# Releasing the store of one batch on its own data: the tail of a batched transposed matmul

## The chip, the cores and the metric

The kernel runs on one core of a Trainium2 chip. The metric is the device time of one execution in microseconds (us), as the median of several executions. The profiled execution has its own span, which is about 1.8 us shorter than the device time, as it begins and ends at the first and last instruction. All positions "at 112.2 us" are counted from the start of that span. PE is the matmul engine (PEld its weight loads), DVE and ACT copy and convert, SyncE (SP) and ACT issue transfers, and 16 DMA engines carry them out. A semaphore is a counter that one engine raises and another waits for. A store has landed when the last of its 16 parts has been confirmed.

## The reference

```python
batch, m, k, n = 16, 512, 512, 512          # a: (16, k, m), b: (16, n, k), float32
out = np.matmul(a.transpose(0, 2, 1), b.transpose(0, 2, 1)).astype(np.float32)
```

The inputs are 16.8 MB each and the output is 16.8 MB: 50.33 MB cross between HBM (the memory of the chip) and SBUF (the working memory of the core).

## The kernel before: the parts that matter

Each batch is multiplied on PE in two halves of two quarters; each finished quarter adds 1 to `summed`, so quarter q (from 0) of batch i brings it to 4*i + q + 1. DVE copies the first half out of PSUM (where PE accumulates), ACT the second. Batches are stored in pairs of 2 MB; only the last pair (batches 14 and 15) is stored as two transfers of 1 MB. The last three pairs are issued by SyncE:

```python
MO, B, H, TAIL = 4, 16, 8, 3
def run_sp(sp):
    ...                                            # cut: all loads
    for j in range(H - TAIL, H - 1):               # pairs 5 and 6
        sp.wait_ge(summed, MO * (2 * j + 2) + 3)
        store(sp, j)
    sp.wait_ge(summed, MO * (B - 1) + 3)           # third quarter of batch 15
    store(sp, H - 1, slice(0, 1))                  # batch 14
    sp.wait_ge(last_go, 3)                         # the three last copies
    store(sp, H - 1, slice(1, 2))                  # batch 15
```

Waiting for quarter 3 of the next batch is an indirect way of waiting for the copies: PE can begin the second half of batch 15 only when ACT has freed that accumulator.

```python
def run_act(act):
    cast_a(act, 0)
    for i in range(B - 1):
        cast_a(act, i + 1)
        copy_out(act, i, slice(2, 4), oa_go)       # oa_go: PE may reuse the accumulator
        ...                                        # cut: stores of the earlier pairs
    copy_out(act, B - 1, 2, last_go)
    copy_out(act, B - 1, 3, last_go)
```

## Time and profile before

| what | value |
|---|---|
| median of the first 3 runs | 124.81 us (124.78 to 124.95) |
| span of the profiled run | 123.1 us |
| PE, DVE, ACT busy | 70%, 46%, 38% |
| DMA share from 4.00 to 120.60 us | 1.01, at 426 GB/s |
| last three stores, issue | 108.26, 114.93, 116.46 us |

How to read it: no compute engine comes near 100%, while the DMA share stays at 1. The lines of the profile are shown in the prediction.

### The profile page before, as it was taken

The numbers are of one execution on the slowest core, as the hardware profiler recorded it, in microseconds if no ns is written. First come the engines' busy times: TensorE is split into PE (matmuls) and PEld (weight loads), VectorE is DVE, ScalarE is ACT, GpSimd is POOL, SyncE is SP. The second block draws the span as 40 slices with busy tenths as digits, with TensorE's granted clock in tenths as the row PEclk, the third lists the DMA queues.
The fourth block names the chain that finished last, engine by engine and source line by source line (L and its number), as shares of the span: only waits on it lengthen the run. The fifth ranks groups of instructions, "written<-read, shape, count | busy, mean of one in ns | idle before, by whom it ended". The sixth has DMA issues, their size and how long they took to land. (4 is left out here: it accounts for less than half of the span.)

```text
span 123.1 us, 1084 instructions
## 1 busy us (share of the span) xinstructions
PE 85.9 (70%) x400; PEld 49.6 (40%) x400; DVE 56.4 (46%) x48; ACT 46.8 (38%) x34; POOL 0.7 (1%) x6
## 2 busy tenths in 40 slices
PE   0007497997999799769932599965992679979600
PEld 0007354643754564436402336533550526447200
DVE  0025377469295665907049007780719306162100
ACT  4004209438617903276300860329230590740300
POOL 2000000000000000000000000000000000000000
PEclk9999999999999999999995558999999558999985
DMA  4999999999999999999999999999999999999993
GB/s 96 389 399 453 407 426 461 434 383 461 426 391 461 426 341 431 429 431 439 437 407 426 445 429 415 429 423 434 463 397 431 423 426 426 429 426 431 426 421 130
DMA packets 5648, 50.33 MB, mean 409 GB/s; under 512 B 528, under 2 KB 528, under 8 KB 528
## 3 DMA queue, kind: packets, MB, share of 16 engines
q1 hardware_dynamic: 4288, 39.85, 77.4%
q10 hardware_dynamic: 1360, 10.49, 20.1%
HBM read 33.55 MB, written 16.78 MB: 409 GB/s over the span
## 5 line engine op out<-in xcount | busy, mean ns | idle before, releaser
L215 PE MATMUL o_ps<-bt_sb,a_bf 128*128 128x512 bf16 x256 | 65.0, 402 | 7.8 <-PEq L190 7.3
L132 ACT CAST a_bf<-a_sb 128x2048 bf16<-128x2048 f32 x16 | 30.4, 1901 | 40.5 <-DMA a_sb<-in_a_dram 40.5
L215 PEld LDWEIGHTS o_ps<-bt_sb,a_bf 128*128 128x128 bf16 x256 | 28.5, 115 | 38.1 <-issue 15.7
L201 PE MATMUL bt_ps<-identity,b_bf 128*128 128x128 f32 x144 | 24.1, 322 | 22.2 <-PEq L190 22.2
L141 DVE COPY o_sb<-o_ps 128x1024 f32<-128x1024 f32 x16 | 19.6, 1224 | 36.5 <-PE o_ps L215 36.5
L201 PEld LDWEIGHTS bt_ps<-identity,b_bf 128*128 128x128 f32 x144 | 22.2, 212 | 27.6 <-issue 26.6
L149 DVE CAST b_bf<-b_sb 128x2048 bf16<-128x2048 f32 x16 | 19.5, 1222 | 18.5 <-DMA b_sb<-in_b_dram 18.5
L141 ACT COPY o_sb<-o_ps 128x1024 f32<-128x1024 f32 (+1 forms) x17 | 16.3, 962 | 28.2 <-PE o_ps L215 28.2
L158 DVE COPY bt_sb<-bt_ps 128x1024 f32<-128x1024 f32 x16 | 19.5, 1216 | 2.9 <-PE bt_ps L201 2.9
L132 ACT ACT_TABLE_LOAD x1 | 1.3, 1283 | 0.9 <-SPq L51 0.9
L119 POOL TENSOR_SCALAR_AFFINE_SELECT identity<-identity 128x128 f32<-128x128 f32 x1 | 0.3, 292 | 0.2 <-POOL identity L117 0.2
L117 POOL MEMSET identity<- 128x128 f32 x1 | 0.2, 204 | 0.7 <-SPq L51 0.7
L261 POOL MEMSET const-bfloat16-1.0<- 128x1 bf16 x1 | 0.1, 101 | 0.0
L261 POOL MEMSET const-uint8-127<- 128x1 uint8 x1 | 0.1, 101 | 0.0
L261 POOL MEMSET const-float32-0.0<- 128x1 f32 x1 | 0.1, 98 | 0.2 <-issue 0.2
L261 POOL MEMSET const-float32-1.0<- 128x1 f32 x1 | 0.1, 98 | 0.0
## 6 DMA issues: line engine op xcount, KB each, us to landing
b_sb<-in_b_dram SPq DMA_DIRECT2D x8, 2048.0 KB, 20.5
a_sb<-in_a_dram SPq DMA_DIRECT2D x16, 1024.0 KB, 17.4
out_dram<-o_sb ACTq DMA_DIRECT2D x5, 2048.0 KB, 15.2
out_dram<-o_sb SPq DMA_DIRECT2D x2, 2048.0 KB, 13.8
out_dram<-o_sb SPq DMA_DIRECT2D x2, 1024.0 KB, 5.1
```

Source lines behind the costliest of these rows:

```text
L117: pool.memset(identity[:], 0.0).then_inc(id_go, 1)
L119: pool.affine_select(out=identity[:], in_=identity[:], compare_op=mybir.AluOpType.not_equal, fill=1.0, base=0, pattern=[[-1, P]], channel_ ...
L132: act.copy(a_bf[i % 2][:], a_sb[s][:]).then_inc(ac_go, 1)
L141: copy(o_sb[i // 2 % OUTS][:, i % 2, rm, :], o_ps[h][:, p, :]).then_inc(go, 1)
L149: dve.tensor_copy(b_bf[:, r, :], b_sb[p % PAIRS][:, r, :]).then_inc(bc_go, n)
L158: dve.tensor_copy(bt_sb[g][:].rearrange("p j (ni r) -> p j ni r", r=NR), bt_ps[:].rearrange("p j r (g ni) -> p g j ni r", g=2)[:, g],).the ...
L201: last = pe.transpose(bt_ps[:, j, r, :], w[:, r, j, :], identity[:])
L215: last = pe.matmul(o_ps[h][:, q, :], a_r[:, rk, 2 * h + q, :], bt_h[:, rk // 2, rk % 2, :], start=(rk == 0), stop=(rk == KO - 1),)
L261: nc = _bacc.Bacc("TRN2", target_bir_lowering=False, num_devices=1)
```

## The change

The intent is to let batch 14's store go as soon as its two copies are done. ACT announces its copy with a drain (an instruction that here ended 0.035 us after the copy before it) and a semaphore. SyncE still waits for one PE count, the first quarter of batch 15, which stands for DVE's copy.

```diff
+        half_go = sem("half_go")
...
-            sp.wait_ge(summed, MO * (B - 1) + 3)
+
+            sp.wait_ge(summed, MO * (B - 1) + 1)
+            sp.wait_ge(half_go, 1)
             store(sp, H - 1, slice(0, 1))
...
+            act.drain().then_inc(half_go, 1)
             copy_out(act, B - 1, 2, last_go)
```

## The prediction

> **What bounds the kernel now.** I read the page from the top down: busy shares, slices, DMA queues, chain, groups. No compute engine is near full (PE 70%, DVE 46%, ACT 38% of 123.1 us). The DMA row of the slices is at 9 from the second slice to the last but one, and the total says why:
>
> ```profile
> PE 85.9 (70%) x400; PEld 49.6 (40%) x400; DVE 56.4 (46%) x48; ACT 46.8 (38%) x34; POOL 0.7 (1%) x6
> ...
> DMA  4999999999999999999999999999999999999993
> ...
> HBM read 33.55 MB, written 16.78 MB: 409 GB/s over the span
> ```
>
> The reader is to see that 50.33 MB have to cross the 16 DMA engines whatever the order, and that the engines hardly rest between the first slice and the last. Over the stretch from 4.00 to 120.60 us the table of windows gives a DMA share of 1.01 and 426 GB/s. 50.33 MB at 426 GB/s are 118.1 us; the remaining 5 us of the span are the start, before the first loads flow (131 GB/s in the half microsecond to 2 us, full rate from 3.5 us), and the end, when the last engines run out and the last store is confirmed. So the DMA is the bound.
>
> The chain that ended last shows only PE 5%: it goes back from the last copy on ACT to 109.97 us and stops there. It leaves out the transfers, so I don't take it as the bound. It is still useful, as it tells what sets the issue of the last store: PE, then ACT's two copies, ending at 115.85 + 0.58 = 116.43 us.
>
> Next the end in order of time (the timeline from 96 us on), as the change acts only there:
>
> ```profile
> 107.36 1.22 DVE L141 COPY o_sb<-o_ps 128x1024 f32<-128x1024 f32 x1 [2.47 <-PE o_ps L215]
> ...
> 109.17 1.01 ACT L141 COPY o_sb<-o_ps 128x1024 f32<-128x1024 f32 x1 [1.05 <-PE o_ps L215]
> ...
> 111.05 1.99 PE L215 MATMUL o_ps<-bt_sb,a_bf 128*128 128x512 bf16 x8
> ...
> 113.82 1.99 PE L215 MATMUL o_ps<-bt_sb,a_bf 128*128 128x512 bf16 x8
> ...
> 115.85 0.58 ACT L141 COPY o_sb<-o_ps 128x512 f32<-128x512 f32 x1 [0.32 <-PE o_ps L215]
> ```
>
> The reader is to see batch 14's output complete at 109.17 + 1.01 = 110.18 us, and the two halves of batch 15's matmuls starting at 111.05 and 113.82. The present store of batch 14 waits until the third quarter of batch 15's matmuls is done, about 113.82 + 1.99/2 = 114.82 us. The rows of the stores, asked for in small windows, place the SyncE issues at 108.26 (batches 12 and 13, 2 MB), 114.93 (batch 14, 1 MB) and 116.46 us (batch 15, 1 MB), with 8.9, 4.7 and 5.6 us to landing, thus landing at about 117.2, 119.6 and 122.1. So the store does sit idle after its data are ready, for 4.7 us. What decides is whether the DMA engines sit idle in that time. Windows of the end (columns: width, busy time of each engine, granted clock, DMA share, GB/s):
>
> ```profile
> 112.00:113.00 1.00, 1.00 (x7) 0.62 (x6) 0.00 (x0) 0.00 (x0) 0.00 (x0) 1.00 0.99 418
> 113.00:114.00 1.00, 1.00 (x10) 0.94 (x9) 0.93 (x1) 0.00 (x0) 0.00 (x0) 1.00 1.04 442
> 114.00:115.00 1.00, 1.00 (x6) 0.49 (x5) 0.30 (x1) 0.06 (x1) 0.00 (x0) 1.00 1.03 434
> 115.00:116.00 1.00, 0.81 (x4) 0.19 (x2) 0.00 (x0) 0.68 (x2) 0.00 (x0) 1.00 1.01 426
> 116.00:117.00 1.00, 0.00 (x0) 0.00 (x0) 0.00 (x0) 0.43 (x1) 0.00 (x0) 1.00 1.01 426
> 117.00:118.00 1.00, 0.00 (x0) 0.00 (x0) 0.00 (x0) 0.00 (x0) 0.00 (x0) 1.00 0.98 410
> ...
> 119.00:120.00 1.00, 0.00 (x0) 0.00 (x0) 0.00 (x0) 0.00 (x0) 0.00 (x0) 0.61 1.00 418
> 120.00:121.00 1.00, 0.00 (x0) 0.00 (x0) 0.00 (x0) 0.00 (x0) 0.00 (x0) 0.50 0.91 385
> 121.00:122.00 1.00, 0.00 (x0) 0.00 (x0) 0.00 (x0) 0.00 (x0) 0.00 (x0) 0.50 0.04 16
> ```
>
> The reader is to see that the share stays at 0.98 to 1.04 in every microsecond from 112 to 120, right through the late issue at 114.93. There is no hole for an earlier store to fill.
>
> **What the Trainium skill says.** "DMA: Bandwidth & Descriptors", section "Queues, rings and completion order", says that on each DMA engine the descriptors of one issuing queue are consumed in ring order. The trace agrees as far as landings can show it: the three last stores, all from SyncE, land in issue order, 2.4 to 2.5 us apart, and 1.049 MB in 2.45 us is 428 GB/s, the full rate. "HBM Reference", section "Specifications (TRN2)", says a core streaming alone gets about 425 GB/s, bounded by its 16 DMA engines; the trace's 426 agrees, so there is no faster rate to reach. "Perfetto Trace Analysis", section "DMA Instruction — HWDGE (DVE, Sync)", says that an issue's profiled time is not the data's movement and that the final semaphore write can be long delayed when the target is HBM. Here the issue takes 0.34 us against a landing 5.6 us later, and almost nothing moves after 121 us while the landing comes at 122.1; that confirmation of about a microsecond is not touched by the change.
>
> **The change part by part.**
>
> Removed: the wait for the third quarter of batch 15. In its place stands the wait for the first quarter of batch 15, which implies that DVE's copy of batch 14 is done, since PE can begin that half only when DVE has freed its accumulator. This quarter ends at 111.05 + 1.99/2 = 112.05. With the 0.11 us from matmul to issue that the old wait shows (114.82 to 114.93), the store goes out at about 112.16, that is 2.77 us earlier. It is not 4.7 us earlier, though the copies are done at 110.18, because the new count is also a PE count.
>
> Added: a drain on ACT with a semaphore increment. It begins when the copy of batch 14 ends at 110.18, and ACT's next work is at 114.94, after 4.76 us of idle time put down to PE. Whatever the drain costs under 4 us is hidden there. No row of this profile has its duration; I count 0 on the path. SyncE gets one more wait, met at about 110.3, before the other is.
>
> Moved: only that one issue. The issue of the last store, 116.46, hangs on ACT's last copy at 116.43, which hangs on PE. PE, DVE and ACT do nothing different before it. The order of the instructions on all engines, compared before and after, is the same but for the drain and the wait.
>
> The sum: at 114.93 the engines still have 0.03 + 0.426 + 0.426 + 0.410 + 0.434 + 0.418 + 0.385 + 0.016 = 2.545 MB to move (the windows' rates by their widths; 118 to 119 has 434). Two stores of 1.049 MB are 2.097 MB of it, so 0.448 MB, or 1.05 us at 426 GB/s, lie ahead of batch 14's store when it is issued. An issue needs about that much: the first one of the program, at 0.95 us, has data flowing in the half microsecond after 1.5. So the late issue arrives just in time. The earlier one meets 0.448 + 2.77 x 0.426 = 1.63 MB of backlog, waits 2.77 us longer in line, begins to move data at the same time as before, and lands at about 119.6 again, now 7.4 us after its issue. The last store follows it and lands at about 122.0. Expected saving: 0, with at most some tenths. The generous bound is to let the 0.98 of 117 to 118 become 1.01 and to let all 16 engines end together: 0.03 us, plus the 0.401 MB after 120 moved at 426 GB/s (0.94 us, to 120.94) instead of ending near 121.5. Neither is likely to be caused by the wait; I count 0.05 us.
>
> **The rivals.**
> 1. The store is on the path to the end, and 2.77 us come off (to about 122.0 us). For it: SyncE waits 21.9 us for PE in the end, 6.2 of them before this issue, and the last thing waited for is a store. Against it: the DMA share of 1.0 in those microseconds, and a last store that cannot issue before 116.46 and needs 1.049/0.426 = 2.46 us of transfer and the confirmation anyway.
> 2. A hole of some DMA engines that the mean share hides. Engines that finished their part of the 2 MB store early might have waited for the next one; then the earlier issue evens them out and up to 0.3 us come off. For it: 1.05 us of backlog is a thin margin. Against it: 410 to 442 GB/s throughout.
> 3. A new cost: the drain delays ACT, or two stores queued together slow loads or copies. Against it: 4.76 us of idle time on ACT, and the last load of `a` is already converted at 106.21, so no load is left to delay. It would add 0 to 0.3 us.
>
> **The range and the chances.** The three runs of before span 124.78 to 124.95, so repeats differ by 0.17 us. From 124.81 less 0.05 I predict 124.8 us. Rival 2 and the repeats set the low end at 124.4, rival 3 and another chip the high end at 125.2. Within 2% means 122.3 to 127.3, which no rival but the first leaves, and it needs the idle DMA time that the windows deny: faster 0.01, same 0.98, slower 0.01.
>
> **What would show each step right or wrong.** Right: the store of batch 14 issued near 112.2 with about 7.4 us to landing, the DMA share still 1.0 in each microsecond to 120, the last issue near 116.5 with 5.5 us to landing, ACT's last copies in place, span near 123.1. Wrong: a landing of batch 14's store well before 119 or of the last one before 121.5 (then there was a hole), a higher rate than 430 GB/s in the end, or ACT's copy after the drain starting late.

## The result, and the profile after

The changed kernel takes 124.85 us (median of 6 runs, 124.66 to 125.05), the kernel before 124.88 us in 6 runs beside and before them. The ratio is 0.9995 with a 95% interval of 0.9976 to 1.0015. Ratios here and below are the mean time of one kernel's fast runs over that of the other's fast runs of the same rounds, so they are not quite the ratio of the medians quoted. Executions over 1.5% slower than the fastest of the same kernel are left out of the means. The result is correct.

The page of the changed kernel, busy shares and DMA slices:

```profile
PE 86.1 (70%) x400; PEld 49.7 (40%) x400; DVE 56.4 (46%) x48; ACT 46.8 (38%) x34; POOL 0.7 (1%) x6
...
DMA  4999999999999999999999999999999999999992
```

The same picture as before: the busy shares are equal, and the DMA row is the same digit for digit but for the last slice. The timeline of the end:

```profile
109.27 1.01 ACT L144 COPY o_sb<-o_ps 128x1024 f32<-128x1024 f32 x1 [1.05 <-PE o_ps L219]
...
111.14 1.99 PE L219 MATMUL o_ps<-bt_sb,a_bf 128*128 128x512 bf16 x8
...
115.93 0.59 ACT L144 COPY o_sb<-o_ps 128x512 f32<-128x512 f32 x1 [0.32 <-PE o_ps L219]
```

Everything sits 0.1 us later than in the earlier trace and in the same order; ACT's last copy is not delayed by the drain. The waits of SyncE in the end (what waited, for whom: us in total, times, longest):

```profile
SPq L276 <- DMA out_dram<-o_sb: 4.6, 1, 4.6
SPq L86 <- ACT o_sb L144: 3.9, 1, 3.9
SPq L111 <- ACTq L188: 1.6, 1, 1.6
```

The third line is the new wait. It runs from the end of the issue before, 108.35 + 0.39 = 108.74, so it is met at about 110.3 (the trace's own row of this wait starts at 110.34), 0.06 us after ACT's copy ended at 109.27 + 1.01 = 110.28. The drain costs no more than that. The store then waits for the first quarter and is issued at 112.24 us, against 114.93 before. It needs 7.2 us to land instead of 4.7. Thus it lands at about 119.5 instead of 119.6, and the last store at 121.9 instead of 122.1. The DMA engines in this time (columns: stretch, width, busy time of PE, PEld, DVE, ACT and POOL, granted clock, DMA share, GB/s):

```profile
115.00:116.00 1.00, 0.89 (x4) 0.22 (x2) 0.00 (x0) 0.66 (x2) 0.00 (x0) 1.00 1.01 426
116.00:117.00 1.00, 0.00 (x0) 0.00 (x0) 0.00 (x0) 0.51 (x1) 0.00 (x0) 1.00 0.99 418
117.00:118.00 1.00, 0.00 (x0) 0.00 (x0) 0.00 (x0) 0.00 (x0) 0.00 (x0) 1.00 1.03 434
...
120.00:121.00 1.00, 0.00 (x0) 0.00 (x0) 0.00 (x0) 0.00 (x0) 0.00 (x0) 0.50 0.70 295
121.00:122.00 1.00, 0.00 (x0) 0.00 (x0) 0.00 (x0) 0.00 (x0) 0.00 (x0) 0.50 0.04 16
```

They were full before and are full now, until 120 us. The lower share after 120 (0.70 against 0.91) goes with an end 0.1 us earlier; the other two profiled runs of this kernel, e1_after and e12_again, end 0.15 us later and 0.14 us earlier than the kernel before, so no gain is to be read from it. The 2.7 us by which the store was issued earlier have become 2.5 us more in line.

### The profile page after: what moved, and what is told of

Read it like the earlier page. It is cut to its first block, busy times and chain, and to the rows that moved or that the text cites. A ratio compares the mean times of both kernels' runs of the same rounds, so it can differ in the third digit from the quotient of the medians.

```text
span 123.0 us, 1086 instructions
## 1 busy us (share of the span) xinstructions
PE 86.1 (70%) x400; PEld 49.7 (40%) x400; DVE 56.4 (46%) x48; ACT 46.8 (38%) x34; POOL 0.7 (1%) x6
```

## The experiments

The theory: at this point stores are waiting in line at full DMA engines, so the issue time of one more changes only how long it queues, until it comes so late that the line runs empty. Rivals: the issue bounds the end (every microsecond counts); single DMA engines have hidden holes that the earlier issue fills; the wait is felt nowhere at all. Twelve kernels ran, in four groups (sections 2 and 3 are one), each group with its own runs of the kernel before; only the last group, e12_again, was compared with the eleven runs of the group before it and one more.

### 1. Where the store is issued

The changed kernel was timed again (e1_after). In e2_copies the store waits for its two copies alone: DVE, too, announces its copy with a drain, after its last turn (the copy of transposed `b` that follows its copy of batch 14).

```diff
-            sp.wait_ge(summed, MO * (B - 1) + 1)
-            sp.wait_ge(half_go, 1)
+            sp.wait_ge(half_go, 2)
...
                 turn(p, 1)
+                if p + 1 == H:
+                    dve.drain().then_inc(half_go, 1)
```

> The changed kernel again, timed beside the other wait positions. Theory (the DMA engines always have a backlog at this point, so the issue only changes the wait in line): ratio to before 1.000, within 0.002; the store of batch 14 issued near 112.2 and landing near 119.5. Rival (hidden holes of single DMA engines, evened out by the earlier issue): a ratio of 0.997 to 0.999, clear of 1.

> The store waits for nothing but its two copies (no count of PE): issue near 110.4, 4.5 us before the old one. Theory: ratio 1.000 again, landing still near 119.5, some 9 us after the issue. Rival of hidden holes: at least as much gain as the changed kernel. Rival that the issue bounds the end: another 1.8 us off.

Two further kernels move the wait the other way, e3_fourth by one quarter and e4_with_last to the condition of the last store:

```diff
-            sp.wait_ge(summed, MO * (B - 1) + 3)
+            sp.wait_ge(summed, MO * (B - 1) + 4)    # e3_fourth
+            sp.wait_ge(last_go, 3)                  # e4_with_last
```

> The wait of before moved one quarter of matmuls later (fourth instead of third): issue near 115.95 instead of 114.93. Theory: the backlog of 1.05 us at 114.93 is used up near 116.0, and a store needs up to 1 us from issue to first data, so a hole of about 0.5 to 0.9 us opens and the time grows by that, to about 125.5. Rival that the wait is not felt at all: 124.85. Rival that every microsecond of the wait counts: plus 1.0.

> The store of batch 14 waits for the same count as the last store: issue near 116.5, 1.5 us later than before. Theory: first data near 117.4 against a backlog that ends near 116.0, so 1.4 us of hole and 126.2 us, ratio about 1.011; the windows show a DMA share well under 1 in 116 to 118. Rival that the wait is not felt: 1.000.

Issue and landing are those of each profiled run; the kernel before of this group had a median of 125.05 us (11 runs). One of the six runs of e4_with_last counts as slow and is left out of its ratio.

| kernel | issued | landed | DMA gap before its data | median us | ratio (95%) |
|---|---|---|---|---|---|
| e2_copies | 109.96 | 119.4 | none | 125.08 | 1.0008 (0.9982 to 1.0035) |
| e1_after | 110.82 | 119.8 | none | 124.76 | 0.9979 (0.9956 to 1.0002) |
| e3_fourth | 116.26 | 120.2 | 0.65 us | 125.15 | 1.0001 (0.9973 to 1.0028) |
| e4_with_last | 116.71 | 120.6 | 1.0 us | 126.13 | 1.006 (1.001 to 1.011) |

Between 110 and 115 us the issue time is worth nothing in these executions: the landing stays at 119.4 to 119.8, and going on from the changed kernel to the two copies alone gains nothing either. Later than that, the line runs empty. Windows of e3_fourth, then of e4_with_last (a packet is counted whole in the stretch in which it starts, so a short stretch can show a share over 1 and a GB/s figure that no engine reached):

```profile
115.00:116.00 1.00, 1.00 (x6) 0.39 (x4) 0.00 (x0) 0.58 (x1) 0.00 (x0) 1.00 0.80 336
116.00:116.50 0.50, 0.23 (x2) 0.00 (x0) 0.00 (x0) 0.23 (x1) 0.00 (x0) 1.00 0.05 16
116.50:117.10 0.60, 0.00 (x0) 0.00 (x0) 0.00 (x0) 0.35 (x1) 0.00 (x0) 1.00 0.00 0
117.10:117.30 0.20, 0.00 (x0) 0.00 (x0) 0.00 (x0) 0.00 (x0) 0.00 (x0) 1.00 1.58 655
```

```profile
116.55:117.55 1.00, 0.00 (x0) 0.00 (x0) 0.00 (x0) 0.14 (x1) 0.00 (x0) 1.00 0.00 0
```

Here one sees how close the old wait was. The engines begin to run out before 116 us and all stand still until 117.10, which is 0.84 us after the issue at 116.26. In e4_with_last they stand still from 116.55 to 117.55, again 0.84 us after the issue. Applied to the kernel before, data could start at 114.93 + 0.84 = 115.77 us (an estimate). The 16 parts of the store in front land from 116.27 to 117.11 us in that trace; as data ended 0.49 us before their landing in e3_fourth and e4_with_last, the DMA engines ran out of it from about 115.78 to 116.62 us (an estimate too). The late issue was thus in time for the first of them, with nothing to spare.

A later issue is felt less than this suggests. Against the kernel before, the store is issued 1.33, 1.78 and 2.36 us later in e3_fourth, e4_with_last and e10_late_pe_before (section 4). The 16 parts of the last store land 1.08, 1.54 and 2.11 us later on average, so some 0.25 us of each delay were free; but its last data end only 0.73, 1.17 and 1.74 us later, so 0.6 us were free at the end. The difference is in the evenness of the engines: after a gap of all of them, the parts of the last store land within 0.2 us of one another, against 0.85 us in the kernel before. These are single profiled executions, and those without a gap end within 0.3 us of one another, so the 0.6 is rough.

Two expectations were missed in size. The gap of e3_fourth does not show in its ratio. Its six runs span 124.67 to 125.46, and the profiled one is the slowest of them; the runs without a profile may well have had no gap, which no record here shows. In e4_with_last the profiled run gained 1.0 us of gap, not 1.4. The ratio of e1_after, 0.9979, lies a hair outside the 0.002 that the theory allowed, in the range of the hidden holes, but its interval reaches 1; section 5 comes back to it.

e1_after also brought evidence. PE happened to run 1.4 us ahead in it (ACT's last copy began at 114.50 instead of 115.93), so its last store was issued at 115.11 instead of 116.54. The span was 123.2 us all the same, and the store took 7.1 us to land instead of 5.4. In this execution, an earlier issue of the last store is worth nothing either. What put PE ahead: the matmuls at 99 us ran while the granted clock was low in the kernel before (0.53 from 95 to 100 us), but not in e1_after. The first line is of the kernel before, the second of e1_after:

```profile
99.10 3.40 PE L215 MATMUL o_ps<-bt_sb,a_bf 128*128 128x512 bf16 x8 [1.65 <-PEq L190]
99.17 1.99 PE L219 MATMUL o_ps<-bt_sb,a_bf 128*128 128x512 bf16 x8 [1.74 <-PEq L194]
```

### 2. The same change with no line in front

In e5_hole_before and e6_hole_after the 2 MB store of batches 12 and 13 is left out of both kernels (their output is wrong), so that nothing waits in line when the store of batch 14 is issued.

```diff
-            for j in range(H - TAIL, H - 1):
+            for j in range(H - TAIL, H - 2):
...
-            sp.reg_mov(all_stored, 16 * STORED)
+            sp.reg_mov(all_stored, 16 * (STORED - 1))
```

> The kernel before without the 2 MB store of batches 12 and 13 (their output is wrong on purpose), so that no backlog lies ahead of the store of batch 14. Theory: the DMA engines run dry near 111.5; the store of batch 14 is issued at about 114.9, its data start near 115.9, and with 2.1 MB at 426 GB/s (4.9 us) the transfers end near 120.8 instead of 121.5: about 0.7 us faster than before, though 5 us of transfer are gone.

> The changed kernel without the same 2 MB store (output wrong on purpose). Theory: the store of batch 14 moves at once, near 113.2 to 115.6, the last one alone from 117.5 to 119.9; 1.5 us faster than before and 0.8 us faster than the run with the old wait and without the 2 MB store. So the earlier wait is worth something once there is no backlog. Rival that the DMA is not what hides it: both equal.

With the old wait the median was 124.44 us, with the new one 123.60 us, with 124.88 for the kernel before in the same group. The runs of e5_hole_before spread over 122.61 to 125.25 us, and three of the six count as slow only because one was so fast; its ratio of 0.987 rests on the other three. By these fast runs alone, the two kernels do not differ (means 123.60 and 123.62 us). All six runs each give 0.84 us by the medians, where 0.8 was expected, and 0.70 us by the means (124.33 and 123.62), and five of the six of e5_hole_before are above every run of e6_hole_after. So the times suggest a gain and do not settle it; the profiled pair, 124.12 and 123.49 us, shows where one comes from. Windows with the old wait, then with the new one:

```profile
111.30:115.80 4.50, 4.50 (x24) 2.61 (x22) 1.22 (x1) 0.59 (x1) 0.00 (x0) 1.00 0.00 0
115.80:116.20 0.40, 0.03 (x1) 0.00 (x0) 0.00 (x0) 0.33 (x1) 0.00 (x0) 1.00 1.32 553
```

```profile
111.70:113.35 1.65, 1.65 (x9) 0.93 (x8) 0.00 (x0) 0.00 (x0) 0.00 (x0) 1.00 0.00 0
113.35:116.00 2.65, 2.65 (x17) 1.64 (x15) 1.23 (x1) 0.59 (x1) 0.00 (x0) 1.00 0.96 396
116.05:117.65 1.60, 0.12 (x1) 0.00 (x0) 0.00 (x0) 0.59 (x1) 0.00 (x0) 1.00 0.01 5
```

With an idle DMA the earlier wait shortens the gap from 4.5 to 1.65 us, but a second gap of 1.6 us then opens before the last store, which PE and ACT release. In this pair of executions the last data end 0.66 us earlier. So the wait changes the transfers once there is no line, and even then the last issue limits what it is worth.

### 3. What bounds the end: one issue, or the bytes

In e7_late_last three spare ACT copies delay the last store of the changed kernel; in e9_less_early one batch of the first pair is not stored (wrong), 1.049 MB less some 80 us before the end.

```diff
             copy_out(act, B - 1, 3, last_go)
+            for x in range(3):                                     # e7_late_last
+                act.copy(spare[:, x, :], o_ps[1][:, 1, :]).then_inc(last_go, 1)
...
-            sp.wait_ge(last_go, 3)
+            sp.wait_ge(last_go, 6)
```

```diff
-                    store(act, j)                                  # e9_less_early
+                    store(act, j, slice(0, 1) if j == 0 else slice(0, 2))
```

> The changed kernel with three more ACT copies of 128x512 (0.5 us each) ahead of the last store: its issue moves from 116.5 to about 118.0. Theory: the stores in line end near 118.6 and the issue needs up to 1 us to first data, so about 0.9 us of the 1.5 are free and 0.3 to 0.6 us are felt. Rival that the last issue bounds the end: plus 1.5 us.

> The changed kernel storing only the first batch of the first pair (batch 1 missing, wrong on purpose): 1.049 MB less near 40 us, nothing else. Theory (bytes at 426 GB/s set the time from start to end): 2.46 us less, ratio 0.980. Rival (the chain of PE and ACT at the end sets it): under 0.5 us less.

e7_late_last: 125.38 us, 0.50 us more than the median of the kernel before (ratio 1.0033, 1.0000 to 1.0066). The three copies took 1.57 us, the first beginning before the copy ahead of it had ended, and put the issue off by 1.46 us (from 117.41, an estimate, to 118.87), so about 1.0 us of the delay was free; but the issue fell at 118.87, not 118.0, as PE was late in this run as well. Its windows show the DMA engines idle from 118.80 to 119.70, the same 0.84 us after the issue.

e9_less_early: 122.28 us (4 runs), 2.60 us less (ratio 0.9789, 0.9760 to 0.9819), against 2.46 expected for 1.049 MB at 426 GB/s. Bytes taken out 80 us before the end come off the end in full. That is what a DMA bound from start to end means. This run alone does not rule out PE and ACT as the limit of the end, since the loads came earlier as well: ACT's last copy began at 114.04 us instead of 115.93 in the changed kernel, and the last store was issued at 114.65 instead of 116.54. e1_after, where that issue was early by itself, speaks against it.

### 4. A PE that comes late, and the cost of the drain

The first group suggested that the old wait stands near the edge. In e10_late_pe_before and e11_late_pe_after two spare DVE copies ahead of DVE's last turn (the expectation calls it the last but one) delay PE's end in both kernels; results stay right.

```diff
+                if p + 1 == H:
+                    for _ in range(2):
+                        dve.tensor_copy(spare[:], bt_sb[0][:])
+                        dve.drain()
                 turn(p, 1)
```

> The kernel before with two spare DVE copies (128x1024) ahead of its last turn but one, so that PE's last matmuls come about 1.2 us (1 to 2.4) later; the result stays right. Issue to first data was 0.84 us in five gaps of the earlier runs. Theory: the store of batch 14 goes out near 116.2, its data start near 117.0, while the stores in line end between 115.9 and 116.6: a gap of 0.5 us or more in all DMA engines, and 0.4 to 1.5 us on the time. Rival that the old wait costs nothing anywhere: no gap and no more than the other late kernel.

> The changed kernel with the same two spare DVE copies. Theory: the store of batch 14 goes out near 113.4, long before the stores in line end, so no gap there; the last store goes out near 117.7 and its data could start at 118.5, about when batch 14's end (118.4 to 119.1), so no gap or one of 0.2 us. Time within 0.3 us of the kernel before, and 0.4 us or more under the other late kernel.

> Sixteen drains on ACT in place of one. Theory: a drain with nothing in flight costs some tens of ns, so the wait of SyncE for the drain ends under 1.5 us later than in the changed kernel (there 0.05 us after ACT's copy), ACT's next copy is not late (4.7 us idle), and the time is the same, near 124.85.

With the old wait 127.19 us (1.0188, 1.0154 to 1.0221), with the new one 126.44 us (1.0138, 1.0104 to 1.0172; one of six runs counts as slow). The difference of 0.75 us is of the expected kind and size, but the two intervals overlap a little. Against the kernel before, the old wait lost 2.4 us, more than the 0.4 to 1.5 expected. The windows show a gap that the new wait does not have. Old wait, then new:

```profile
116.00:116.60 0.60, 0.60 (x5) 0.41 (x5) 0.60 (x1) 0.00 (x0) 0.00 (x0) 1.00 0.04 14
116.60:118.10 1.50, 1.50 (x7) 0.57 (x5) 0.06 (x1) 0.59 (x1) 0.00 (x0) 1.00 0.00 0
```

```profile
116.00:117.00 1.00, 1.00 (x6) 0.46 (x5) 0.00 (x0) 0.45 (x1) 0.00 (x0) 1.00 0.99 418
117.00:118.00 1.00, 0.42 (x2) 0.00 (x0) 0.00 (x0) 0.68 (x2) 0.00 (x0) 1.00 1.06 451
118.00:119.00 1.00, 0.00 (x0) 0.00 (x0) 0.00 (x0) 0.04 (x1) 0.00 (x0) 1.00 0.42 172
```

With the old wait all engines idle for 1.5 us from 116.60; with the new one they are full until 118. My expectation that the new one would be as fast as the kernel before failed, by 1.6 us. After 118 the share drops to 0.42: the last store, released by the late PE, is late itself. The change protects against one of the two gaps only. The profiled run of the new wait is the fastest of its six (125.17 us, with PE 0.7 us ahead of the other profile at the last copy); what cost its other runs another 0.8 us and more has no profile, so that part of the 1.6 us is not shown.

The run with sixteen drains (e8_drains) waits for them until 109.98 + 2.1 = 112.1 us, about 0.6 us after ACT's copy ended at 111.51; the changed kernel's one drain took 0.06. That makes roughly 0.03 us a drain (an estimate, 0.5 us over 15, from waits given to a tenth). The rows of the fifteen added drains agree: after the first, which takes in the copy that it waits for, they are 8 to 14 ns long and begin 33 ns apart (shortest, median and longest in ns):

```profile
L189 ACTq DRAIN  x15: 8/8/1041, 110.5 to 112.0; - x15
```

ACT's next copy was not late: it began after 4.74 us of idle time put down to PE. The one timed run of 125.38 us is at the slow end of what the kernel before shows (124.65 to 125.34 in that group); a single run can't say more.

### 5. Is there a small gain after all?

The first 12 runs of the changed kernel all stayed at or below 125.05 us, which the kernel before did not. So it was run once more. (The expectation miscounts: 8 of the first 28 runs of the kernel before lie above 125.05 us, not 11.)

> The changed kernel once more, as its first 12 runs all stayed at or below 125.05 us while 11 of the first 28 or so of the kernel before lay above that. If the earlier store takes away a gap that the old wait has in executions with a late PE, none of these six is above 125.2 and the ratio is 0.996 to 0.999. If that was chance (the run with the store earlier still had three of six above 125.1), they spread up to 125.4 like those of before, and the ratio is 1.000 within 0.002.

The median was 124.84 us (124.75 to 125.29), the ratio 1.0008 (0.9986 to 1.0030). Two of the six were above 125.2. The lead in the first 12 was chance, as far as these runs go. The three comparisons gave 0.9995, 0.9979 and 1.0008: no gain is resolved. The widest interval leaves room for 0.44%, the other two for 0.24% and 0.14%.

## Why the prediction was right

- **The bound.** "The DMA is the bound" held. Removing 1.049 MB 80 us before the end took off 2.60 us, and an issue of the last store 1.4 us earlier took off nothing.
- **The issue and the landing.** The store was expected at about 112.16 and was issued at 112.24; 7.4 us to landing were expected and 7.2 measured.
- **The sum.** A saving of 0.05 us was counted; the medians differ by 0.03 us, inside the noise, so that the two agree says nothing. The sum of what was left to move (2.545 MB, of it 0.448 ahead of the store) is right. One reading is off, without consequence: 106.21 us is when the conversion of the last load begins, not when it is done. And the sign of being wrong "a higher rate than 430 GB/s" was badly chosen, as the windows of its own trace had 442 and those of the changed kernel have 434.
- **The backlog.** Confirmed by the issue times: from 109.96 to 114.93 us the landing stays, and after that a gap opens. From the other side it is only suggested: with the store in front left out, the same change shortens the gap in the traces, and the times give 0.7 to 0.8 us over all runs but nothing over the fast runs.
- **The drain.** Counted as 0 on the path; SyncE saw it 0.06 us after the copy, in idle time.
- **A term mis-sized, without consequence.** The prediction took the time from issue to first data to be "about that much", 1.05 us. The program's first load does take 1.01 us (0.95 to 1.96), but the stores after a gap take 0.84, so the line had 0.2 us more to spare than it said, and 0.6 us before the end of the last data moved (section 1). "Just in time" was true of the first engines only. The confirmation of "about a microsecond" was too large as well: in the record of DMA packets the last data of the kernel before end at 121.57 us, 0.5 us ahead of the landing.
- **The rivals.** The first fell with the unchanged end. The hole of single DMA engines is not seen: e2_copies, which could fill it just as well, had a ratio of 1.0008, and the earlier issue evened nothing out: the parts of the last store land over 0.85 us in the kernel before and over 0.98 us in the changed one. The third, a new cost, was not seen either.
- **Left open.** Whether the kernel before has a small gap in its slower executions (125.2 to 125.6 us) could not be seen, as only one of its executions has a profile. Why the runs of e5_hole_before spread so much more than those of e6_hole_after was not settled either.

## What to carry to other kernels

Before moving a store's wait, ask whether the DMA engines stand idle between the earliest possible issue and the present one: a store that joins a full line a few microseconds earlier only waits longer in it. Such a wait has a slack of about the backlog in front less the time from issue to first data, here 1.05 less 0.84 us; within it the change is worth nothing, beyond it a late issue opens a gap. That is the slack of the average engine; the end of the transfers was moved only after 0.6 us here, since the engines ended more evenly after a gap. If the transfers fill the whole span, only fewer bytes or a shorter start and end make the kernel faster.

## What the Trainium skill lacked or had wrong

- "DMA: Bandwidth & Descriptors", section "Latency and other measured facts", gives about 600 ns to the first byte for a transfer of the kind that SyncE issues, and doesn't say from where it counts. From the start of the profiled issue to the first packet after a gap, the record of DMA packets shows 0.83 to 0.85 us in seven gaps of six runs (one each in e3, e4, e5, e7 and e10, two in e6); from the end of the issue it is 0.49 to 0.50 us. All seven are stores.
- "Perfetto Trace Analysis", section "Sequencer-only Instruction (DRAIN, etc)", gives no duration for a drain, and no page has one for a drain of the kernel's own on ACT. On ACT with nothing left to do, one took 0.06 us at most until SyncE saw it, and sixteen begin 0.03 us apart.
- "TensorE: Matmul & The Clock Gate", section "What's actually happening", says the clock's activity window is free-running, so that the point at which the clock speeds up varies by some 500 ns. Here the granted clock of the kernel before was 0.53 from 95 to 100 us, while e1_after had its dip from 85 to 90 us (0.51) and none from 90 to 110. The eight matmuls at 99 us took 3.40 us in the first and 1.99 in the second; the last copies of e1_after came 1.4 us earlier, and the span was the same within 0.2 us, as the DMA bounds it. That such a dip moves the end of PE by over a microsecond from one execution to the next, and so the edge at which a late store is felt, the page doesn't say.
- No page found says how far apart the 16 parts of one store land: those of a 1 MB store land within 0.2 us of one another after a gap of all engines (e3, e4, e5, e6, e7, e10), and over 0.85 to 1.09 us at the end of an unbroken flow (the kernel before, the changed one, e1, e2, e12).
